# RoPE on half of each head row: the untouched half copied from DRAM to DRAM, the rotated half alone through SBUF in 128-byte runs

## The chip, the cores and the metric

One NeuronCore of one Trainium2 chip. The metric is device time in microseconds (us). Times are medians of a few executions, most of them within 0.3% of each other. Several cores are not involved; the granted clock was 1.0 in every run below.

## The reference

`x` has shape (16, 512, 16, 64) = (batch, seq, heads, dim), fp32, 33.5 MB. Only the first 32 of the 64 columns are rotated; the other 32 pass through.

```python
x1, x2 = x[..., :32], x[..., 32:]            # x2 is not touched
c, s = cos[None, :, None, :16], sin[None, :, None, :16]
rotated_first  = x1[..., :16] * c - x1[..., 16:] * s
rotated_second = x1[..., :16] * s + x1[..., 16:] * c
out = concatenate([rotated_first, rotated_second, x2], axis=-1)
```

A head row is 64 fp32 values, 256 B: 128 B to rotate, 128 B to pass on. There are 131,072 head rows.

## The kernel before

Each of 16 tiles is one batch entry. A partition holds 4 sequence positions of 16 heads, 16 KB that are contiguous in DRAM, so a load and a store move one run of 16 KB per partition. The rotation happens in place in the tile; the second half of each row simply rides along.

```python
    xf = x.rearrange("b (p k) h d -> b p (k h d)", p=P)      # P = 128, K = 4
    of = out.rearrange("b (p k) h d -> b p (k h d)", p=P)
    # ... x_pool has 6 buffers; cos and sin are spread over the heads by GpSimd ...
    for b in range(B):
        x_t = x_pool.tile([P, K, H, D], fp32)
        nc.sync.dma_start(out=x_t.rearrange("p k h d -> p (k h d)"), in_=xf[b])
        # ...
        x12 = x_t.rearrange("p k h d -> p (k h) d")[:, :, 0:HF]
        nc.vector.tensor_mul(out=a_t[:], in0=x12, in1=cc_op)
        nc.vector.tensor_mul(out=b_t[:], in0=x12, in1=ss_op)
        # ... one subtract and one add of 16 columns each, back into x12 ...
        nc.scalar.dma_start(out=of[b], in_=x_t.rearrange("p k h d -> p (k h d)"))
```

## Time and profile before

| | before |
|---|---|
| time | 163.29 us (163.12 to 163.46) |
| span of the profiled run | 161.4 us |
| bytes through the DMA queues | 33.56 MB loads + 33.56 MB stores |
| 16 DMA engines, share of the span | 49.4% + 48.5% |
| VectorE busy | 108.7 us |

From the page of the kernel before, parts 2, 3 and 5. The two rows of part 2 are 40 equal slices of the span: mean busy share of the 16 DMA engines in tenths (9 is 90% or more), and the rate. The rows of part 3 are a queue's packets, MB, and the time that its packets took as a share of 16 engines' span (q1 carries the loads, q10 the stores). The row of part 5 is a group of instructions: count, busy us, mean ns, then the idle time before them and what ended it.

```profile
DMA  5999999999999999999999999999999999999994
GB/s 162 430 414 447 414 382 443 414 430 447 418 434 434 422 443 430 418 451 422 426 443 422 430 434 430 434 434 418 447 422 426 451 414 428 439 422 438 430 422 195
...
q1 hardware_dynamic: 2304, 33.56, 49.4%
q10 hardware_dynamic: 2304, 33.56, 48.5%
...
L64 DVE TENSOR_TENSOR a_t<-x_t,CCX 128x2048 f32<-128x2048 f32 x16 | 37.0, 2313 | 42.1 <-DMA x_t<-in_x_dram 30.1
```

The DMA engines are full in 38 of 40 slices at about 430 GB/s, and VectorE waits for loads (30.1 us). The kernel is as long as its bytes. The DMA records in the trace hold 4096 data packets of 16,384 B with a median of 611 ns: 4096 x 0.611 / 16 = 156 us.

### The profile page before, as it was taken

To read this page: it belongs to the slowest core of one execution; us is meant where nothing else is said; L and a number is where in the kernel's file an instruction comes from. 1 tells how busy PE (TensorE), PEld (TensorE's weight loads), DVE (VectorE), ACT (ScalarE), POOL (GpSimd) and SP (SyncE) were. 2 spreads that over 40 slices of the span, in tenths; PEclk is the share of its full clock that TensorE was granted. 3 is DMA by queue.
4 is the path that set the end of the run, shared out by engine and by line. 5 is a ranking of instruction groups with operands and counts; after the bars stand their busy time and mean duration, and the time that the engine had idled before them with its cause. 6 is when DMAs were issued, how large, how long until landed. Compare 5 with 4: busy or idle time off the path is not lost.

```text
span 161.4 us, 189 instructions
## 1 busy us (share of the span) xinstructions
DVE 108.7 (67%) x64; POOL 6.0 (4%) x14
## 2 busy tenths in 40 slices
DVE  0009999999995692947839296592957939389400
POOL 3090000000000000000000000000000000000000
DMA  5999999999999999999999999999999999999994
GB/s 162 430 414 447 414 382 443 414 430 447 418 434 434 422 443 430 418 451 422 426 443 422 430 434 430 434 434 418 447 422 426 451 414 428 439 422 438 430 422 195
DMA packets 4673, 67.25 MB, mean 417 GB/s; under 512 B 544, under 2 KB 544, under 8 KB 576
## 3 DMA queue, kind: packets, MB, share of 16 engines
q1 hardware_dynamic: 2304, 33.56, 49.4%
q10 hardware_dynamic: 2304, 33.56, 48.5%
q0 software_dynamic: 64, 0.13, 0.2%
q14 instruction: 1, 0.01, 0.0%
HBM read 33.69 MB, written 33.55 MB: 417 GB/s over the span
## 4 chain that ended last, share of the span: by engine, by line
DMA 60%; DVE 28%; POOL 2%; issue 2%; DVEq 1%; POOLq 0%; SPq 0%; PEldq 0%
DMA out_dram<-x_t 31%; DMA x_t<-in_x_dram 25%; DVE a_t L64 9%; DVE b_t L65 8%; DVE x_t L66 6%; DVE x_t L72 5%; DMA cosL<-in_cos_dram 4%; POOL CCX L49 1%; DVEq L105 1%; POOL SSX L50 1%; POOLq L105 0%; SPq L57 0%; DVEq L66 0%; PEldq L105 0%
## 5 line engine op out<-in xcount | busy, mean ns | idle before, releaser
L64 DVE TENSOR_TENSOR a_t<-x_t,CCX 128x2048 f32<-128x2048 f32 x16 | 37.0, 2313 | 42.1 <-DMA x_t<-in_x_dram 30.1
L65 DVE TENSOR_TENSOR b_t<-x_t,SSX 128x2048 f32<-128x2048 f32 x16 | 36.5, 2283 | 0.0
L66 DVE TENSOR_TENSOR x_t<-a_t,b_t 128x1024 f32<-128x1024 f32 x16 | 19.5, 1220 | 0.2
L72 DVE TENSOR_TENSOR x_t<-a_t,b_t 128x1024 f32<-128x1024 f32 x16 | 19.5, 1218 | 0.0
L49 POOL COPY CCX<-cosL 128x512 f32<-128x512 f32 x4 | 2.4, 612 | 5.4 <-DMA cosL<-in_cos_dram 5.4
L50 POOL COPY SSX<-sinL 128x512 f32<-128x512 f32 x4 | 2.4, 614 | 0.1
L39 POOL DMA_DIRECT2D cosL<-in_cos_dram x1 | 0.7, 668 | 0.8 <-PEq L105 0.8
L40 POOL DMA_DIRECT2D sinL<-in_sin_dram x1 | 0.5, 534 | 0.0
L94 POOL MEMSET const-float32-0.0<- 128x1 f32 x1 | 0.1, 98 | 0.2 <-issue 0.2
L94 POOL MEMSET const-bfloat16-1.0<- 128x1 bf16 x1 | 0.1, 101 | 0.0
L94 POOL MEMSET const-uint8-127<- 128x1 uint8 x1 | 0.1, 101 | 0.0
L94 POOL MEMSET const-float32-1.0<- 128x1 f32 x1 | 0.1, 98 | 0.0
## 6 DMA issues: line engine op xcount, KB each, us to landing
x_t<-in_x_dram SPq DMA_DIRECT2D x16, 2048.0 KB, 20.3
out_dram<-x_t ACTq DMA_DIRECT2D x16, 2048.0 KB, 23.4
cosL<-in_cos_dram POOLq DMA_DIRECT2D x1, 64.0 KB, 6.6
sinL<-in_sin_dram POOLq DMA_DIRECT2D x1, 64.0 KB, 7.1
```

Source lines behind the costliest of these rows:

```text
L39: nc.gpsimd.dma_start(out=cosL[:], in_=cosf)
L40: nc.gpsimd.dma_start(out=sinL[:], in_=sinf)
L49: nc.gpsimd.tensor_copy(out=dst_c, in_=src_c)
L50: nc.gpsimd.tensor_copy(out=dst_s, in_=src_s)
L64: nc.vector.tensor_mul(out=a_t[:], in0=x12, in1=cc_op)
L65: nc.vector.tensor_mul(out=b_t[:], in0=x12, in1=ss_op)
L66: nc.vector.tensor_tensor(out=x12[:, :, 0:Q], in0=a_t[:, :, 0:Q], in1=b_t[:, :, Q : 2 * Q], op=mybir.AluOpType.subtract,)
L72: nc.vector.tensor_tensor(out=x12[:, :, Q : 2 * Q], in0=a_t[:, :, Q : 2 * Q], in1=b_t[:, :, 0:Q], op=mybir.AluOpType.add,)
L94: nc = _bacc.Bacc("TRN2", target_bir_lowering=False, num_devices=1)
L105: with _tile.TileContext(nc) as tc:
```

## The change

The intent is to move fewer bytes through the DMA engines. A byte that goes in and out of SBUF passes an engine twice; a byte copied from DRAM to DRAM passes it once: the queues moved 33.56 + 33.56 MB in the kernel before. So 3 x 16.78 = 50.3 MB instead of 67.1 MB. The price: a load, a copy and a store each touch every second 128 B of DRAM.

```diff
-    xf = x.rearrange("b (p k) h d -> b p (k h d)", p=P)
-    of = out.rearrange("b (p k) h d -> b p (k h d)", p=P)
+    K = 8
+    T = B * S // (P * K)                                   # 8 tiles in place of 16
+    xh = xf.rearrange("t p (r d) -> t p r d", d=D)
+    oh = of.rearrange("t p (r d) -> t p r d", d=D)
     # ... cos/sin table: two small loads and four VectorE copies in place of GpSimd's; one a_t and b_t buffer, not four ...
-        nc.sync.dma_start(out=x_t.rearrange("p k h d -> p (k h d)"), in_=xf[b])
+        x_t = x_pool.tile([P, K, H, HF], fp32)
+        nc.sync.dma_start(out=x_t.rearrange("p k h d -> p (k h) d"), in_=xh[t, :, :, 0:HF])
+        nc.sync.dma_start(out=oh[t, :, :, HF:D], in_=xh[t, :, :, HF:D])
     # ... the same four VectorE operations, now on two halves of a tile ...
-        nc.scalar.dma_start(out=of[b], in_=x_t.rearrange("p k h d -> p (k h d)"))
+        nc.scalar.dma_start(out=oh[t, :, :, 0:HF], in_=x_t.rearrange("p k h d -> p (k h) d"))
```

More of the change, by code (lines that the diff above doesn't have):

```diff
@@ L20 @@
     fp32 = mybir.dt.float32
+    P = 128
     B, S, H, D = x.shape
@@ L24 @@
     HF = D // 2
-    P = 128
-    K = S // P
-    xf = x.rearrange("b (p k) h d -> b p (k h d)", p=P)
-    of = out.rearrange("b (p k) h d -> b p (k h d)", p=P)
-    cosf = cos.rearrange("(p k) j -> p (k j)", p=P)
-    sinf = sin.rearrange("(p k) j -> p (k j)", p=P)
+    K = 8
+    T = B * S // (P * K)
+    PB = S // K
+    REP = P // PB
+    xf = x.rearrange("b s h d -> (b s h d)").rearrange("(t p f) -> t p f", t=T, p=P)
+    of = out.rearrange("b s h d -> (b s h d)").rearrange("(t p f) -> t p f", t=T, p=P)
@@ L33 @@
+    xh = xf.rearrange("t p (r d) -> t p r d", d=D)
+    oh = of.rearrange("t p (r d) -> t p r d", d=D)
+    cosf = cos.rearrange("(p k) j -> p (k j)", k=K)
+    sinf = sin.rearrange("(p k) j -> p (k j)", k=K)
     const_pool = ctx.enter_context(tc.tile_pool(name="const", bufs=1))
     x_pool = ctx.enter_context(tc.tile_pool(name="xp", bufs=6))
-    ab_pool = ctx.enter_context(tc.tile_pool(name="abp", bufs=4))
-    cosL = const_pool.tile([P, K, HF], fp32)
-    sinL = const_pool.tile([P, K, HF], fp32)
@@ L39 @@
-    nc.gpsimd.dma_start(out=cosL[:], in_=cosf)
-    nc.gpsimd.dma_start(out=sinL[:], in_=sinf)
-    CCX = const_pool.tile([P, K, H, 2, Q], fp32)
-    SSX = const_pool.tile([P, K, H, 2, Q], fp32)
-    for k in range(K):
-        dst_c = CCX[:, k].rearrange("p h c j -> p (h c) j")
-        dst_s = SSX[:, k].rearrange("p h c j -> p (h c) j")
-        src_c = cosL[:, k : k + 1, 0:Q].to_broadcast((P, 2 * H, Q))
-        src_s = sinL[:, k : k + 1, 0:Q].to_broadcast((P, 2 * H, Q))
-        nc.gpsimd.tensor_copy(out=dst_c, in_=src_c)
-        nc.gpsimd.tensor_copy(out=dst_s, in_=src_s)
@@ L52 @@
-    cc_op = CCX.rearrange("p k h c j -> p (k h) (c j)")
-    ss_op = SSX.rearrange("p k h c j -> p (k h) (c j)")
-    for b in range(B):
-        x_t = x_pool.tile([P, K, H, D], fp32)
-        nc.sync.dma_start(out=x_t.rearrange("p k h d -> p (k h d)"), in_=xf[b])
-        a_t = ab_pool.tile([P, K * H, HF], fp32)
-        b_t = ab_pool.tile([P, K * H, HF], fp32)
-        x12 = x_t.rearrange("p k h d -> p (k h) d")[:, :, 0:HF]
-        nc.vector.tensor_mul(out=a_t[:], in0=x12, in1=cc_op)
-        nc.vector.tensor_mul(out=b_t[:], in0=x12, in1=ss_op)
-        nc.vector.tensor_tensor(
-            out=x12[:, :, 0:Q],
-            in0=a_t[:, :, 0:Q],
-            in1=b_t[:, :, Q : 2 * Q],
-            op=mybir.AluOpType.subtract,
-        )
-        nc.vector.tensor_tensor(
-            out=x12[:, :, Q : 2 * Q],
-            in0=a_t[:, :, Q : 2 * Q],
-            in1=b_t[:, :, 0:Q],
-            op=mybir.AluOpType.add,
-        )
-        nc.scalar.dma_start(out=of[b], in_=x_t.rearrange("p k h d -> p (k h d)"))
+    ab_pool = ctx.enter_context(tc.tile_pool(name="abp", bufs=1))
@@ new lines @@
+    stage = const_pool.tile([PB, 2, K, HF], fp32)
+    nc.scalar.dma_start(out=stage[:, 0].rearrange("p k j -> p (k j)"), in_=cosf)
+    nc.scalar.dma_start(out=stage[:, 1].rearrange("p k j -> p (k j)"), in_=sinf)
+    table = const_pool.tile([P, 2, K, 2, Q], fp32)
+    for r in range(REP):
+        for t in range(2):
+            nc.vector.tensor_copy(
+                out=table[r * PB : (r + 1) * PB, t],
+                in_=stage[:, t, :, 0:Q].unsqueeze(2).to_broadcast((PB, K, 2, Q)),
+            )
@@ new lines @@
+    C = table[:, 0].rearrange("p k c j -> p k (c j)")
+    Sn = table[:, 1].rearrange("p k c j -> p k (c j)")
+    KC = 4
+    for t in range(T):
+        x_t = x_pool.tile([P, K, H, HF], fp32)
+        nc.sync.dma_start(out=x_t.rearrange("p k h d -> p (k h) d"), in_=xh[t, :, :, 0:HF])
+        nc.sync.dma_start(out=oh[t, :, :, HF:D], in_=xh[t, :, :, HF:D])
+        for k0 in range(0, K, KC):
+            x1 = x_t[:, k0 : k0 + KC, :, 0:HF]
+            c = C[:, k0 : k0 + KC].unsqueeze(2).to_broadcast((P, KC, H, HF))
+            s = Sn[:, k0 : k0 + KC].unsqueeze(2).to_broadcast((P, KC, H, HF))
+            a_t = ab_pool.tile([P, KC, H, HF], fp32)
+            b_t = ab_pool.tile([P, KC, H, HF], fp32)
+            nc.vector.tensor_mul(out=a_t[:], in0=x1, in1=c)
+            nc.vector.tensor_mul(out=b_t[:], in0=x1, in1=s)
+            nc.vector.tensor_sub(
+                out=x1[:, :, :, 0:Q], in0=a_t[:, :, :, 0:Q], in1=b_t[:, :, :, Q:HF]
+            )
+            nc.vector.tensor_add(
+                out=x1[:, :, :, Q:HF], in0=a_t[:, :, :, Q:HF], in1=b_t[:, :, :, 0:Q]
+            )
+        nc.scalar.dma_start(out=oh[t, :, :, 0:HF], in_=x_t.rearrange("p k h d -> p (k h) d"))
```

## The prediction

> **What bounds the kernel now.** The 16 DMA engines. The slice view shows DMA busy at 90% or more in 38 of 40 slices. The queue view: 33.56 MB on the load queue (49.4% of 16 engines' span) and 33.56 MB on the store queue (48.5%), 97.9% together. VectorE is busy 108.7 of 161.4 us, and its largest wait is for loads (30.1 us, waits view). The DMA records of the trace hold 4096 data packets of 16384 B, median 611 ns: 4096 x 0.611 / 16 = 156 us, which is the kernel. Head and tail cost about 5 us.
>
> **Intent.** Half of each row no longer goes in and out of SBUF, so bytes through the engines fall from 67.1 MB (2 x 33.55) to 50.3 MB (3 x 16.78). At today's rate that would be 117 us of DMA.
>
> **What it adds.** Every run becomes 128 B: 131,072 head rows, each with one load, one store and one DRAM-to-DRAM run, 393,216 runs in place of 4096, or 24,576 per engine. Cost of a run, worked out from the trace: a completion packet of 4 B took 9 ns, a 4096 B packet 159 ns, a 16384 B packet 611 ns; this fits about 8.4 ns fixed plus 36.8 ns per KB. So 128 B is an estimated 13 ns[...]: 24,576 x 13 ns = 320 us if each run pays the fixed part and the engines are always busy.
>
> [...] Downward: several runs could share a packet's fixed part (the 4096 B packet holds eight 512 B runs).
>
> **Other parts.** VectorE keeps its work: 16 half-tiles x (2.3 + 2.3 + 1.2 + 1.2 us) = 112 us[...]: off the critical path. The table set-up moves from GpSimd (first multiply now at 11.95 us) to four small VectorE copies, under DMA work. Loads shrink from 16 issues to 8; copies add 8.
>
> **Critical path.** All of the added run cost lies on it, as DMA is already at 98%. [...]with some weight on the unseen costs I predict **390 us**, range **290 to 600**. Faster by over 2%: 0.01; within 2%: 0.01; slower by over 2%: 0.98.
>
> **What would show it right.** DMA busy share near full over the middle, queue bytes over time near 130 GB/s, some 393,000 runs under 512 B, landing times well above 20 us, VectorE at about 30% and waiting for loads, the chain of waits nearly all DMA. A load run and a store run near 13 ns in the DMA records[...].
>
> **What would make it wrong.** Runs merged into larger packets (117 to 200 us);[...] a copy run much slower than the other two.

The sum came to 375 us: 320 us for the runs, 15 us for head, last multiply and last store, and 40 us more for the copies. Another 15 us of weight for costs that I could not see in the trace made it 390 us; those costs were also the reason for the far upper end of the range.

## The result

| | before | after |
|---|---|---|
| time | 163.29 us (163.12 to 163.46) | 267.42 us (267.23 to 267.60) |
| ratio after / before | | 1.637 (1.634 to 1.640) |
| bytes through the DMA queues | 67.1 MB | 50.5 MB |
| DMA packets | 4673 | 393,761 |
| mean rate over the span | 417 GB/s | 190 GB/s |
| VectorE busy | 108.7 us | 110.8 us |

A ratio is the mean time of one kernel's fast runs over that of the other's fast runs of the same rounds, so it is not quite the ratio of the medians quoted.

The change is slower, as forecast, but 267 us lies below the forecast range of 290 to 600 us: the short runs cost less than I had thought.

From the page of the kernel after, the same parts, and part 6 (issues: count, KB each, median us from issue to landing). Here q1 carries loads and copies, q10 the stores.

```profile
DMA  8999999999999999999999999999999999999999
GB/s 142 209 181 164 218 217 180 174 174 212 218 206 176 181 218 210 174 174 181 218 218 195 174 185 218 202 174 174 191 218 217 187 160 203 218 194 174 174 174 127
DMA packets 393761, 50.47 MB, mean 190 GB/s; under 512 B 393632, under 2 KB 393760, under 8 KB 393760
...
q1 hardware_dynamic: 262400, 33.56, 97.7%
q10 hardware_dynamic: 131360, 16.91, 48.4%
...
L68 DVE TENSOR_TENSOR a_t<-x_t,table 128x2048 f32<-128x2048 f32 x16 | 36.7, 2292 | 132.2 <-DMA x_t<-in_x_dram 131.9
...
x_t<-in_x_dram SPq DMA_DIRECT2D x8, 2048.0 KB, 28.3
out_dram<-in_x_dram SPq DMA_DIRECT2D x8, 2048.0 KB, 34.3
out_dram<-x_t ACTq DMA_DIRECT2D x8, 2048.0 KB, 23.5
```

First, the queue shares add to 146% of 16 engines' span. A packet's time is what it took from its own start to its own end, so packets of one engine overlap. In the kernel before the shares added to 98%: with 611 ns packets the overlap cannot be seen.

Second, the rate does not wander; it sits on two levels, 218 and 174 GB/s. Stretches of the kernel after (us from the span's start; length; VectorE and GpSimd busy; clock; DMA share; GB/s):

```profile
35.00:39.00 4.00, 0.00 (x0) 0.00 (x0) 1.00 1.38 218
255.00:260.00 5.00, 0.00 (x0) 0.00 (x0) 1.00 1.65 174
```

With 16 engines and 128 B, 218 GB/s is one run per engine every 9.4 ns, and 174 GB/s one every 11.8 ns. From the time stamps of the DMA records, the 128 B runs cover 261 us; of their half-microsecond bins, some 44% lie within 0.35 ns of 9.41 ns and 46% within 0.35 ns of 11.76 ns, which are the values that I use below. The kinds can be told apart too: the SP queue takes loads and copies in turns, so a packet's rank in it says which it is, and the ACT queue has the stores. Bins with loads alone (74) or loads beside stores (167) have a median of 9.41 ns; bins with copies alone (142), stores alone (42) or copies beside stores (91) have one of 11.75 to 11.76 ns.

The records themselves (number, median and 90th percentile of a packet's own duration, ns):

```
before  16384 B  4096    611   615      4 B  9
after     128 B  393216   13    24      4 B  9
```

So the predicted 13 ns is exactly the median duration of a 128 B packet. It is not the time after which the engine starts the next one, 9.41 or 11.76 ns.

### The profile page after: what moved, and what is told of

It is laid out like the page before. It is cut to its first block, busy times and chain, and to the rows that moved or that the text cites. A ratio compares the mean times of both kernels' runs of the same rounds, so it can differ in the third digit from the quotient of the medians.

```text
span 265.5 us, 157 instructions
## 1 busy us (share of the span) xinstructions
DVE 110.8 (42%) x68; POOL 0.2 (0%) x4
## 2 busy tenths in 40 slices
DMA packets 393761, 50.47 MB, mean 190 GB/s; under 512 B 393632, under 2 KB 393760, under 8 KB 393760
## 3 DMA queue, kind: packets, MB, share of 16 engines
q1 hardware_dynamic: 262400, 33.56, 97.7%
## 4 chain that ended last, share of the span: by engine, by line
SPq 53%; DMA 35%; DVE 5%; DVEq 0%; issue 0%
DMA x_t<-in_x_dram 35%; SPq L61 29%; SPq L60 24%; DVE a_t L68 2%; DVE b_t L69 2%; DVE x_t L70 1%; DVE x_t L73 0%; DVEq L102 0%; DVEq L68 0%
## 5 line engine op out<-in xcount | busy, mean ns | idle before, releaser
L68 DVE TENSOR_TENSOR a_t<-x_t,table 128x2048 f32<-128x2048 f32 x16 | 36.7, 2292 | 132.2 <-DMA x_t<-in_x_dram 131.9
L69 DVE TENSOR_TENSOR b_t<-x_t,table 128x2048 f32<-128x2048 f32 x16 | 36.6, 2284 | 0.0
L50 DVE COPY table<-stage 64x256 f32<-64x256 f32 x4 | 1.1, 286 | 4.6 <-DMA stage<-in_cos_dram 3.1
## 6 DMA issues: line engine op xcount, KB each, us to landing
out_dram<-x_t ACTq DMA_DIRECT2D x8, 2048.0 KB, 23.5
```

Of the source, the lines that this page charges most:

```text
L50: nc.vector.tensor_copy(out=table[r * PB : (r + 1) * PB, t], in_=stage[:, t, :, 0:Q].unsqueeze(2).to_broadcast((PB, K, 2, Q)),)
L68: nc.vector.tensor_mul(out=a_t[:], in0=x1, in1=c)
L69: nc.vector.tensor_mul(out=b_t[:], in0=x1, in1=s)
```

## The experiments

Fifteen kernels ran. Theories at the start:

- **A, overlap.** Each DMA engine starts a 128 B run 9.41 ns after the last one, or 11.76 ns if all the runs in flight write DRAM. My 13 ns was a duration, not an interval.
- **B, supply.** The making of descriptors sets the pace, and each run costs the same.
- **C, alignment.** Runs that read the second half of a 256 B row are the slow ones; no trace had shown this.
- **D, a step:** writes to DRAM in short runs carry a cost that longer runs do not have; no trace had shown this either. **E:** a limit shared by all engines. **P:** the cost belongs to a packet and could be shared by several runs.

Blocks with a + or - below are shortened; where words stand after the +, they sum up a small test program and are not its code. The loop of the change in short: `load(t)` on the SP queue, `copy(t)` on SP, VectorE, `store(t)` on the ACT queue.

### phased: one kind of transfer at a time

```diff
-    for t in range(T):                # load, copy, rotate, store
+    for t in range(T): load(t)        # 8 tile buffers
+    for t in range(T): copy(t)
+    for t in range(T): rotate(t); store(t)   # store on the SP queue too
```

> All loads, then all copies, then all stores, on the one SP queue; result correct. Theory A (an engine starts the next 128 B run 9.41 ns after the last, although one run takes 13 ns, and 11.76 ns after it when the runs in flight all write DRAM): loads at 217 GB/s for 77 us, copies and stores both at 174 GB/s for 96 us each, about 277 us in all. Theory B (the supply of descriptors sets the pace, every run costs the same): one rate in all three phases. Theory C[...]: copies slower than stores, stores as fast as loads.

280.99 us, ratio 1.722 (1.719 to 1.724), correct. The rate row of its page, loads first:

```profile
GB/s 148 193 217 195 201 215 192 200 217 196 203 218 185 173 176 171 174 171 173 175 171 177 174 174 174 174 174 174 174 174 174 174 174 174 174 174 174 172 176 123
```

Loads reach 217 (with a dip where one load follows another), copies and stores hold 174. That is theory A's picture. Theory B wanted one rate; C wanted copies slower than stores. It also shows what the mix in the change is worth: a store that runs beside loads costs 9.41 ns, not 11.76 (the bins of the kernel after), and phased, which separates them and puts the stores on the SP queue, takes some 14 us more in all.

### whole_load: a third of the short runs taken away

```diff
-        x_t = x_pool.tile([P, K, H, HF], fp32)
-        nc.sync.dma_start(out=x_t..., in_=xh[t, :, :, 0:HF])
+        x_t = x_pool.tile([P, K, H, D], fp32)          # 4 buffers
+        nc.sync.dma_start(out=x_t..., in_=xf[t])       # whole rows, contiguous
```

> Loads take the whole row in one contiguous run per partition; copies and stores stay 128 B; result correct. Theory A:[...] 262 to 282 us. Theory B (descriptor supply): a third of the runs is gone, so about 265 x 2/3 = 177 us plus, at most 210 us.

277.16 us, ratio 1.698 (1.696 to 1.701), correct. It is not faster than the change at all, which ends B: 263,713 packets in place of 393,761, and no gain. The rate row:

```profile
GB/s 307 351 176 261 448 157 174 174 267 459 164 174 174 275 459 156 174 174 277 459 155 174 174 303 416 172 174 174 319 391 181 174 174 317 394 180 174 174 174 118
```

The slices with loads now reach 459 GB/s (a load packet holds 32 KB and counts whole in the slice in which it starts, so single slices read high), and the loads are soon over; what is left, copies and stores, runs alone at 174. Loading half a row as a 128 B run takes an engine 9.4 ns. In the kernel before, 16,384 B took 611 ns; at that rate the 256 B of a whole row take 9.5 ns, as long. Leaving out half the row on a load saves nothing.

### long_runs: everything of the change but its runs

```diff
+        nc.sync.dma_start(out=x_t..., in_=xf[t])       # whole rows, 4 buffers
-        nc.sync.dma_start(out=oh[t, :, :, HF:D], in_=xh[t, :, :, HF:D])
+        nc.scalar.dma_start(out=of[t], in_=x_t...)     # whole rows
```

> Everything else of the change kept (8 tiles, table, VectorE work, single a/b buffers), but whole rows loaded and stored in contiguous runs and no copies; result correct. Theories A, B and C: back to the time before, 160 to 168 us. If it stays well above, something else than the runs costs time.

163.00 us, ratio 0.999 (0.996 to 1.002), correct. The new tiling, table, half-tile VectorE work and single a_t and b_t buffers cost nothing. The whole loss is in the runs.

### no_copy: the copies left out

```diff
-        nc.sync.dma_start(out=oh[t, :, :, HF:D], in_=xh[t, :, :, HF:D])
```

> The copies left out (second half of each output row is not written, wrong on purpose). Theory A: 16,384 runs per engine, loads paired with stores at 9.41 ns, 154 us, plus 12 to 25 us of head, tail and unpaired stretches: 166 to 182 us. If the copies were much dearer than the other runs[...] it falls below 155 us.

168.72 us, ratio 1.034 (1.032 to 1.036); the output is wrong. The rate row:

```profile
GB/s 93 217 215 184 218 185 217 218 216 217 218 217 218 217 218 218 217 217 217 218 218 217 217 217 218 217 218 219 216 218 217 217 177 174 174 174 174 174 174 91
```

Loads beside stores: 217. Stores alone at the end: 174. The copies of the change thus cost 267.4 - 168.7 = 98.7 us, or 12.0 ns per run and engine (8192 each): near 11.76 ns, and less than my prediction had for them. And note that the load and the store of half of the data, in 128 B runs, already take longer than the load and the store of all of it in 16 KB runs.

### align: where in a 256 B row the run starts

```diff
+ loads: first halves x2, second halves x2
+ copies: first->first x2, second->second x2, second->first x2
+ stores: to first halves x2, to second halves x2;  SBUF->SBUF x2
```

> 128 B runs, phases of two tiles on the SP queue, wrong on purpose: loads from first halves, from second halves; copies first to first, second to second, second to first; stores to first halves, to second halves; SBUF to SBUF. Theory A: alignment does not matter: 217, 217; 174, 174, 174; 174, 174; 217 GB/s.[...]

Theory C had runs from second halves slower than runs from first halves.

187.63 us. Its output is wrong, which doesn't matter for the time. Stretches, in order: loads from first halves, loads from second halves, the three kinds of copies, the two kinds of stores. Columns: GpSimd busy, clock, DMA share, GB/s.

```profile
8.00:12.00 4.00, 0.00 (x0) 1.00 1.38 218
39.00:43.00 4.00, 0.00 (x0) 1.00 1.38 218
50.00:66.00 16.00, 0.00 (x0) 1.00 1.61 174
74.00:88.00 14.00, 0.00 (x0) 1.00 1.60 174
98.00:112.00 14.00, 0.00 (x0) 1.00 1.62 174
120.00:140.00 20.00, 0.00 (x0) 1.00 1.65 174
144.00:160.00 16.00, 0.00 (x0) 1.00 1.65 174
```

Alignment does not show (218 GB/s for both kinds of loads, 174 for all copies and stores), so C falls, and with it the 40 us that the forecast's sum held for the copies. SBUF to SBUF came to 198 to 207 GB/s in its slices, a little under the 217 expected.

### sweep: the length of the run

```diff
+ for L in (64, 128, 256, 512, 1024, 2048): load   2 MB in runs of L
+ for L in ...:                             copy   2 MB in runs of L
+ for L in ...:                             store  2 MB in runs of L     # one queue
```

> 2 MB per phase on the SP queue, no arithmetic, wrong on purpose: loads with runs of 64, 128, 256, 512, 1024, 2048 B, then DRAM-to-DRAM copies, then stores in the same lengths. Theory A[...]: loads near 145, 217, 290, 348, 387, 410 GB/s; copies and stores near 109, 174, 249, 316, 366, 398.[...] My prediction's 8.4 ns fixed part would give 128 B loads 157 GB/s and 512 B loads 300.

The figures of theory A are an estimate. They can be worked out to within 2% from 9.41 ns for a 128 B load and 11.76 ns where DRAM is written (kernel after) and from 611 ns for 16,384 B, 1.19 ns for each 32 B (kernel before): this leaves about 4.6 ns fixed for a load and 2.35 ns more where DRAM is written. Theory D had the shorter copies and stores well below these figures.

195.37 us. Its output is wrong, which doesn't matter for the time. Stretches of its trace, in order: the loads at 128, 256, 512, 1024 and 2048 B, the copies at 64, 128 and 256 B, the stores at 128, 256, 512, 1024 and 2048 B (columns as above):

```profile
24.00:30.00 6.00, 0.00 (x0) 1.00 1.38 218
35.00:40.00 5.00, 0.00 (x0) 1.00 1.34 217
43.00:47.00 4.00, 0.00 (x0) 1.00 1.19 290
50.00:53.00 3.00, 0.00 (x0) 1.00 1.10 348
56.00:59.00 3.00, 0.00 (x0) 1.00 1.05 387
64.00:82.00 18.00, 0.00 (x0) 1.00 1.89 87
88.00:95.00 7.00, 0.00 (x0) 1.00 1.65 174
98.00:103.00 5.00, 0.00 (x0) 1.00 1.26 281
155.00:162.00 7.00, 0.00 (x0) 1.00 1.65 174
166.00:172.00 6.00, 0.00 (x0) 1.00 0.96 218
175.00:178.00 3.00, 0.00 (x0) 1.00 1.01 290
182.00:185.00 3.00, 0.00 (x0) 1.00 1.05 346
188.00:191.00 3.00, 0.00 (x0) 1.00 1.03 385
```

In ns per run and engine (run length x 16 engines / rate): loads 9.4, 18.9, 28.2, 47.1, 84.7 and stores 11.8, 18.8, 28.2, 47.4, 85.1 from 128 to 2048 B. From 256 B up a load or a store cost 9.4 ns and 1.18 ns more for each 32 B. So theory A's 4.6 ns missed there, and the prediction's 8.4 ns was not far off. But at 128 B a load costs 9.4 ns in all, not 14.1, so the fit from 4 KB and 16 KB packets could not be carried down to 128 B. And 64 B copies run at 87 GB/s, again 11.8 ns: from 128 to 64 B the interval of a copy did not shrink. Copies of 256 B took 14.6 ns (281 GB/s), near 4.7 ns and 1.18 ns more for each 32 B, so the 2.35 ns extra of a 128 B copy hardly show there. Stores equal loads from 256 B up (218 against 217 GB/s, then 290 against 290), so no step appears between 256 and 512 B and D falls there. At 128 B a store does cost 2.35 ns more than a load; that something like D is behind this is not ruled out. Copies of 512 B and more wandered between some 180 and 380 GB/s (1 us bins of the DMA records); I did not find out why.

### engines and engines2: per engine, or shared?

```diff
+ copies split over 16, 8 and 4 blocks of rows        # engines
+ the same with gaps between the blocks               # engines2
```

> Only 128 B copies, two tiles each split over 16, then 8, then 4 DMA engines, wrong on purpose. Theory A (each engine's own run cost): 11.76 ns per run and engine throughout: 174, 87, 43.5 GB/s for 24, 48, 96 us. Rival B or E (descriptor supply or DRAM shared by all engines): with fewer engines each gets more; a shared limit of 174 GB/s would leave 8 engines faster than 11.76 ns per run, at 9.41 ns (109 GB/s) or less.

77.97 us, all at 174 GB/s. Its output is wrong, which doesn't matter for the time. The test failed as a test: the queue's share of 16 engines' span stayed at 150% throughout, so all 16 engines still took part (the blocks lie end to end, and I suppose they were treated as one). It says nothing on the question. With gaps:

> The earlier try did not change the number of engines[...], so it told nothing; here the blocks have gaps. Copies of 128 B runs: 32,000 runs over 16 engines, 16,000 over 8, 8,000 over 4, then a load over 16 and the same load as 16 pieces of 8 engines each; wrong on purpose. Theory A[...]: 174, 87, 43.5 GB/s, about 23.5 us for each of the three copy phases. Rival E (a limit that all engines share, in DRAM or in the making of descriptors): with 8 engines more than 87 GB/s[...], or up to 174 if nothing else binds; the copy phases shrink. Loads over 8 engines: 109 GB/s under A, more under E.

127.54 us. Its output is wrong, which doesn't matter for the time. Copies over 16, 8 and 4 engines:

```profile
16.00:23.00 7.00, 0.00 (x0) 1.00 1.63 177
31.00:47.00 16.00, 0.00 (x0) 1.00 0.82 87
52.00:70.00 18.00, 0.00 (x0) 1.00 0.41 44
```

Half the engines move half as much, and the DMA share halves with them. The 11.76 ns belong to each engine (11.6 to 11.8 ns a run in all three stretches); E falls for the copies. The loads in 16 small pieces, meant for 8 engines each, ran at 43 to 61 GB/s, less than either theory said; small DMAs were mixed into that and it settles nothing.

### two_queues: both hardware queues with the same work

```diff
+ 4 tiles loaded, then 8 copied, then 4 stored; tiles alternate between the SP and the ACT queue
```

> 128 B runs with both hardware queues doing the same thing at once: 4 tiles of loads, 8 of copies, 4 of stores; wrong on purpose. Theory A: queues change nothing, 217 GB/s for loads, 174 for copies and stores. Rival B (one queue's descriptor supply is the limit): faster than with one queue, up to 1.5 times or more.

188.64 us. Its output is wrong, which doesn't matter for the time. Loads, copies, stores:

```profile
6.00:40.00 34.00, 0.00 (x0) 1.00 1.38 217
50.00:120.00 70.00, 0.00 (x0) 1.00 1.65 174
140.00:180.00 40.00, 0.00 (x0) 1.00 1.65 174
```

The same levels as with one queue, so B's last form (one queue's supply) falls too. What a second queue did take away are the dips between one load and the next: 217 GB/s over the whole stretch of loads, where phased has 203 (10 to 80 us).

### pool_copy and pool_phases: several runs in one packet

```diff
-        nc.sync.dma_start(out=oh[t, :, :, HF:D], in_=xh[t, :, :, HF:D])
+        for p0 in (0, 64):                              # pool_copy
+            nc.gpsimd.dma_start(out=oh[t, p0:p0+64, :, HF:D], in_=xh[t, p0:p0+64, :, HF:D])
```

> The copies issued on the GpSimd queue, where in the kernel before eight 512 B rows shared a 4096 B packet; result correct. If runs share packets there, the copy packets are 4096 B of 32 runs[...]; but GpSimd took 534 and 668 ns for 128 rows before, about 4 to 5 ns a row, so the 131,072 copy runs should take 550 to 690 us to issue, and the kernel 500 to 750 us.

241.67 us, correct, a single run of unknown state: faster than the change, and 1.48 times the 163.34 us of before on the same chip. I had the issue cost wrong: GpSimd spent 2.6 us on 8192 rows, not 4 ns on each. Runs do share packets here, 4096 B each (32 runs):

```profile
q10 hardware_dynamic: 131360, 16.91, 50.8%
q1 hardware_dynamic: 131200, 16.78, 46.2%
q0 software_dynamic: 4352, 16.78, 29.3%
```

Its rate was 207 to 241 GB/s from the 2nd to the 35th of 40 slices, so the 174 level is mostly gone, but it is nowhere near the 430 GB/s of the kernel before. The next kernel puts every transfer on that queue:

> 128 B loads, copies and stores, 4 tiles each, all on the GpSimd queue, where 32 runs share a 4096 B packet; wrong on purpose. If the cost of a run is a cost of a packet (theory P), a packet takes about 159 ns as in the kernel before and in the bursts of the run with the copies on this queue: near 400 GB/s. If it is a cost of a run whatever the packet (theory R),[...] 174 to 218 GB/s in all three phases, as that run showed in its sustained stretches.

243.05 us for 25 MB, with idle gaps: the DMA engines were busy about half of the time, as each issue waited 6.5 to 8.3 us. Its output is wrong, which doesn't matter for the time. In the DMA records a 4096 B packet of 32 runs took 309 ns at the median (10% took 207 ns or less), against 159 ns for the 4096 B packets of eight 512 B runs in the kernel before. A duration is not an interval, so here are the rates within one copy burst and one store burst (a burst is what one issue moves; columns as in align):

```profile
79.50:84.30 4.80, 0.00 (x0) 1.00 0.95 217
156.20:162.50 6.30, 0.00 (x0) 1.00 0.84 163
```

From first start to last end, bursts of loads and of copies ran at 203 to 213 GB/s, 9.6 to 10.1 ns a run; bursts of stores at 162, 12.6 ns. Sharing a packet did not take the 9.4 ns of a run away, so P falls as a cure. But it did take away most of the 2.35 ns extra of a copy, though all of these runs write DRAM: the 11.76 ns of theory A hold for the SP and ACT queues and not for these copies. The records of pool_copy agree: stretches that are nearly all copies run at about 219 GB/s there, which fits its lead over the change. Why is open, as are the packets of 207 ns.

### dense: 128 B runs without gaps in DRAM

```diff
+ loads of 128 B runs that follow each other in DRAM, into SBUF with gaps
+ copies from gapped to dense DRAM;  stores from gapped SBUF to dense DRAM
```

> 128 B runs, the other side keeping gaps of 128 B, but side by side in DRAM: 4 loads from dense DRAM, then 4 copies from gapped to dense DRAM, then 4 stores to dense DRAM, all on the SP queue; wrong on purpose. If length alone counts: 217 GB/s for the loads, 174 for copies and stores, as with gaps.[...] If descriptors merge on the dense side, the records show it and the rates rise further.

143.09 us. Its output is wrong, which doesn't matter for the time. Loads, then stores:

```profile
6.00:40.00 34.00, 0.00 (x0) 1.00 0.98 207
96.00:138.00 42.00, 0.00 (x0) 1.00 1.65 174
```

The stores stay at 174, and the copies in between at 173 (48 to 90 us): it is the run's length that costs, not the gap. The loads brought a surprise. Their records are 4096 packets of 2048 B, 16 runs read at once, and still the rate stays near 217 GB/s on its plateaus: 151 ns for each packet, 9.4 for every 128 B piece written to SBUF. Here the pace follows the short writes, not the number of reads. (I had expected a merge to raise the rate; it did not.)

### run512, run1024, run2048: the change with longer runs

```diff
-    xh = xf.rearrange("t p (r d) -> t p r d", d=D)        # 128 B + 128 B
+    xh = xf.rearrange("t p (r d) -> t p r d", d=2 * L // 4)   # L bytes through SBUF, L bytes copied
```

The bytes per queue and the VectorE work are the change's. The wrong columns are rotated.

> The change unchanged but for its run: 512 B through SBUF, the next 512 B copied, and so on; same bytes per queue, same VectorE work; wrong on purpose, as the wrong columns are rotated. From the sweep:[...] 164 to 173 us and 7 more: 168 to 182 us, so level with before or a little slower. The prediction's own rule (8.4 ns and 36.8 ns per KB) says 2048 x 3 x 26.8 ns = 165 us plus 7.

> As the 512 B one with runs of 1024 B, wrong on purpose. From the sweep:[...] 140 to 145 us and 7 more, 146 to 155 us: now faster than before, unless DRAM itself binds (33.6 MB read and 33.6 MB written in that time is some 450 GB/s).

> As the others with runs of 2048 B, wrong on purpose. The law that fits 128, 512 and 1024 B[...] gives[...] 409 GB/s, 512 runs x 3 x 80 ns = 123 us, plus 18 us of head and tail as in the 1024 B run (146 us against 130 us of runs): 137 to 143 us. If DRAM itself binds, the rate stays near the 387 GB/s of 1024 B or falls: 146 us or more.

The cost of a run in these forecasts: for 512 B 28.2 ns for a load and a store (sweep) and an assumed 23.5 to 28.2 for a copy, 2048 of each per engine; for 1024 B 47.1 ns for a load and a store (sweep) and an assumed 42.3 to 47.1 for a copy, 1024 of each; for 2048 B the line through the 9.4, 23.5 and 42.3 ns that 128, 512 and 1024 B took in the change, run512 and run1024.

| run | time | ratio to before |
|---|---|---|
| 128 B (the change) | 267.42 us | 1.637 (1.634 to 1.640) |
| 512 B | 160.75 us | 0.985 (0.983 to 0.986) |
| 1024 B | 146.09 us | 0.895 (0.893 to 0.896) |
| 2048 B | 154.80 us | 0.952 (0.947 to 0.956) |

The rate row of the page of run512:

```profile
GB/s 87 304 312 346 320 298 345 348 348 348 347 345 348 348 347 348 342 291 332 347 348 348 347 348 347 348 347 347 349 346 347 348 348 347 348 348 180 44 290 194
```

Of run1024:

```profile
GB/s 74 359 363 319 370 360 380 369 387 387 385 358 380 387 386 383 374 362 387 370 387 387 385 375 379 387 386 386 387 383 386 387 387 386 387 381 84 10 348 222
```

Of run2048:

```profile
GB/s 91 260 379 357 224 354 407 296 371 408 308 332 297 358 410 286 323 387 396 365 363 408 407 411 368 373 396 409 384 335 395 376 377 292 388 326 139 0 305 248
```

In the mix of the real kernel, 348 GB/s is 23.5 ns for 512 B and 387 is 42.3 ns for 1024 B: 4.7 ns and 1.18 ns for each 32 B, and 128 B at 4.7 + 4.7 = 9.4 ns fits the same line. So the intent of the change, fewer bytes, works once the run is long: level with before (under 2%) at 512 B, 10.5% faster at 1024 B. The 512 B run was faster than I expected (168 to 182), as the extra time that the sweep showed for a load and a store (28.2 ns each, 4.7 above the line) appeared only in part. Sorted by kind as above, the records of run512 have loads alone at 28.2 ns and stores alone at 28.2, but copies alone at 23.5, loads beside stores at 23.5 and copies beside stores at 23.5 (medians of half-microsecond bins). The number of queues is not what decides, as copies alone use one queue; why a load or a store alone takes 4.7 ns more is open. The 2048 B run missed its 137 to 143: it reaches 411 GB/s but dips to 224, so the line of the shorter runs gives out there. Whether DRAM itself sets those dips is open; the median includes one slow run of four, the ratio does not. All three show a hole near the end (rates of 44, 10 and 0): the copies are done, and the last store waits for VectorE, which in run1024 gets its last load at 122 us and works until 136 us.

No version that computes the reference beat the kernel before. The arithmetic says why: whole rows through SBUF cost a head row 2 x 256 B, 19.1 ns of an engine at 611 ns for 16,384 B; three 128 B runs cost 28.2 ns (3 x 9.41) to 32.9 ns (9.41 + 2 x 11.76).

## Why the prediction was wrong

- **What bounds the kernel before, right.** The DMA engines, by their bytes. With long runs in the change's structure the time was 163.00 us again.
- **Direction and its cause, right.** 393,216 runs of 128 B, and their cost lies in full on the critical path: the engines were full throughout, VectorE waited 131.9 us for loads, and the rest of the change cost nothing (long_runs).
- **The failed step:** "this fits about 8.4 ns fixed plus 36.8 ns per KB. So 128 B is an estimated 13 ns ...: 24,576 x 13 ns = 320 us". The duration was right to the nanosecond, a median of 13 ns. The multiplication was wrong: the engine starts the next run after 9.41 ns, or 11.76 ns where all runs write DRAM. The 24,576 runs of an engine cover 261 us, 10.6 ns each, in place of 320. A sign was on the page after: queue shares that add to 146%. In the trace before I see nothing that would have shown it: the shares add to 98%, and its short packets are few. Without the 40 us below and the 15 us of weight the sum would still have been 320 + 15 = 335 us, 68 us too high, so this step and not the additions made most of the error.
- **The 40 us more for the copies, wrong.** Loads from second halves ran as fast as those from first halves (218 GB/s). Copies do cost 11.76 ns, but so do stores alone, and so do copies out of first halves (174 GB/s in align).
- **"with some weight on the unseen costs", 15 us, wrong way.** No step showed at 512 B in the sweep (stores at 218, 290 and 346 GB/s for 256, 512 and 1024 B, loads at 217, 290 and 348), and a second queue did not move the two levels. The lower end of the range, 290 us, left no room for overlapped runs, which the prediction never named among what could make it wrong.
- **"queue bytes over time near 130 GB/s"**: 190. **"the chain of waits nearly all DMA"**: 53% was the SP queue held up at its issues and 35% DMA, which I take for the same thing, a queue that waits for the engines: in phased an issue of 16,384 runs took 10.3 us for loads and 12.0 us for copies (medians), close to the engines' 9.6 and 12.0 us for that many.
- **VectorE off the critical path, right**; its share was 42%, not 30%, since the span was shorter.

What stays open: why 128 B runs that all write DRAM take 11.76 ns where others take 9.41, why copies in shared packets do not, why a load or store of 256 B or more takes 4.7 ns more when it runs alone, and why long copies dip.

## What to carry to other kernels

Count DMA work in runs and not only in bytes: in this mix a run of 128 to 1024 B cost an engine 4.7 ns plus 1.18 ns for each 32 B (11.76 ns for 128 B with only writes to DRAM in flight), so a quarter of the bytes saved by cutting rows into 128 B pieces was more than lost (104 us slower); the same saving broke even at runs of 512 B and paid at 1024 B. When you work out a rate from packet times in a trace, check that the packets of an engine don't overlap: a start-to-start interval, or a sum of shares above 100%, tells a duration from a cost. Before you build the real thing, a copy of the kernel with a longer run and a wrong result shows cheaply whether the idea or its run length is at fault.
